# The last stage of a hybrid decoder layer, put into a written order: loads split off, output products by column halves

## The chip, the cores and the metric

The kernel runs on one core of a Trainium2 chip. The metric is the device time of one execution in microseconds (us). The kernel before was timed three times: median 2399.8 us, from 2398.44 to 2401.62. A further, profiled execution took 2395.87 us; the span of its trace, from the first instruction to the last, is 2394.1 us, and the 1.8 us between the two lie around the program.

## The reference, cut to what matters

One layer: RMSNorm, one input projection, two token mixers side by side (a chunked gated DeltaNet and a dilated windowed attention in three groups), gates, an output projection and the residual. Sequence 2048, model width 1024, everything float32. The last part, which the change touches:

```python
o_dn = rms_norm(o_dn, dn_norm_w[layer]) * jax.nn.silu(dn_z.reshape(B, T, DN_HEADS, HEAD_DIM))
y_dn = o_dn.reshape(B, T, DN_WIDTH) @ w_branch_dn[layer]
...
alpha = jax.nn.softmax(jnp.stack(lses, axis=0), axis=0)
o_swa = jnp.sum(alpha[..., None] * jnp.stack(outs, axis=0), axis=0).astype(x.dtype)
o_swa = o_swa * jax.nn.silu(swa_z.reshape(B, T, SWA_HEADS, HEAD_DIM))
y_swa = o_swa.reshape(B, T, SWA_WIDTH) @ w_branch_swa[layer]

g_dn, g_swa = jnp.split(gates, 2, axis=-1)
merged = jax.nn.sigmoid(g_dn) * y_dn + jax.nn.sigmoid(g_swa) * y_swa
x = x + merged @ w_out[layer]
```

## The kernel before, in words

Every large product is done in three matmuls: each float32 operand is split into a high part, rounded to the fp32r format (a ScalarE copy), and a low part, the remainder (a subtract on VectorE or GpSimd), and high times high, low times high and high times low are summed in PSUM. A **split** of a weight piece is therefore two instructions: `w_split` has the copy at L942 (ACT) and the subtract at L944 (DVE, or POOL for some pieces).

The program has three long stretches. First the attention projections and the attention itself. Then the channel units (`cunits`, matmuls L524 to L526), with the DeltaNet inverse and scan laid between them; the last units write the gates to DRAM (L915, L916). Then the **last stage**, from 2011 us on, in `run`: eight blocks of 256 tokens. A block has two parts:

- **branch products** (`fin_y`, eight times, m = 0 to 7, 24 matmuls of 256 columns each, L997 to L999) into a PSUM tile `mm`, of which there are three buffers. What follows each is called its **tail**: gates times sums (L1001, DVE, which also frees the PSUM buffer), the two branches added (L1003, POOL), the high part of the sum (`mh`, L1004, ACT) and its low part (`ml`, L1005, POOL). The gates come by a load `gt`, three buffers.
- **output products** (`fin_out`, four times: two tiles of 128 tokens by two halves of 512 columns, 24 matmuls of 512 columns each, L1014 to L1016), then the residual (L1020, DVE) and the store. Their step k reads `mh` and `ml` of branch product m = k.

Beside them run the preparations for the next block: for each tile of 128 tokens the **merge** (`combine`, L954 to L966: nine small and large DVE steps with one ACT step L956 between) of the three attention groups from a load `oc` of 780 KB with one buffer, and four times `o_prep`: a transpose on PE (L981), a product with the gate path `z` (L982, DVE) and its split (L985 ACT, L986 POOL).

The weights: 16 pieces of the branch weights are loaded and split near the end of the last channel unit (`tail`). 16 pieces of the output weight follow: they take the place of the activations that the last channel unit reads, so they are split from 2012 us on. They come in the order (k0 = 0, m = 0), (k0 = 4, m = 0), (k0 = 0, m = 1) and so on; here p0 to p15. A piece holds 512 rows by 128 columns: `fin_out` of the left half reads p0 to p7 and starts with the even ones, that of the right half p8 to p15. `take(n)` loads n pieces and splits those that are more than three loads old.

`at(d, f)` runs f after d further **hooks**; a hook comes after every sixth matmul of a unit or an output product, and twice in a branch product. It is a place in the program. For the attention (`swa`) the order written is the order run on PE, ACT, DVE and POOL (`manual_schedule`). All that comes later, the last stage too, is handed to a scheduler, which sets the order on every engine. The DMA queue on SP is ordered by it throughout that part.

## Time and profile before

| what | before |
|---|---|
| median of three runs | 2399.8 us |
| profiled execution; its span | 2395.87 us; 2394.1 us |
| PE busy | 2350.5 us (98%) |
| DVE, ACT, POOL busy | 1169.7, 856.6, 824.0 us |
| DMA moved | 307.30 MB, mean 128 GB/s |

PE is TensorE's matmuls, PEld its weight loads, DVE VectorE, ACT ScalarE, POOL GpSimd, SP the engine that issues the DMAs. Times in a row of the timeline are counted from the start of the span: start, length, engine, line, instruction, and in brackets the idle time before it with what ended it. L1014 is line 1014 of the kernel. A matmul's row is longer than its step: the next one starts before it ends.

### The profile page before, as it was taken

The page shows a single profiled execution, that of the slowest core. Times are in us where ns is not written, and L with a number is a line of the kernel's source. Part 1 is how long each engine was busy: PE and PEld are TensorE (multiplying, and loading weights), DVE is VectorE, ACT ScalarE, POOL GpSimd, SP SyncE. Part 2 cuts the span into 40 slices and gives each one's busy share as a digit, 9 for nine tenths or more (in the row PEclk, how much of TensorE's full clock was granted, in tenths as well). Part 3 has the DMA queues.
Part 4 walks back from the last instruction along what each step waited for, and adds up shares of the span by engine and source line. Part 5 has one row for each costly group of instructions (what it writes and reads, how often), then busy time and mean ns, then how long its engine had stood idle before and what let it go on. Part 6 is the DMA issues. An engine that isn't in the chain of part 4 may idle for free.

```text
span 2394.1 us, 40632 instructions
## 1 busy us (share of the span) xinstructions
PE 2350.5 (98%) x13640; PEld 2136.8 (89%) x13640; DVE 1169.7 (49%) x2819; ACT 856.6 (36%) x3021; POOL 824.0 (34%) x1803
## 2 busy tenths in 40 slices
PE   8999999999999999999999999999999999999999
PEld 7899999999999999988777878888888878889988
DVE  5543344334434434344666666999344433454431
ACT  6433333444434444334665662111233313111110
POOL 6633333333333334301442451101233212433441
PEclk9999999999999999999999999999999999999999
DMA  8443344333333335233454443222567645555442
GB/s 283 156 115 111 107 122 120 104 101 108 109 97 111 111 91 128 85 94 103 126 128 117 117 106 118 68 75 75 191 203 207 184 150 158 155 175 161 147 141 75
DMA packets 378808, 307.30 MB, mean 128 GB/s; under 512 B 61352, under 2 KB 345320, under 8 KB 378216
## 3 DMA queue, kind: packets, MB, share of 16 engines
q1 hardware_dynamic: 378312, 304.64, 43.5%
q8 instruction: 108, 1.77, 0.3%
q14 instruction: 100, 0.82, 0.1%
q10 hardware_dynamic: 288, 0.07, 0.0%
HBM read 187.92 MB, written 116.69 MB: 127 GB/s over the span
## 4 chain that ended last, share of the span: by engine, by line
PE 86%; DMA 4%; DVE 3%; POOL 3%; ACT 2%; issue 2%; SPq 0%; ACTq 0%; DVEq 0%; POOLq 0%
PE mm L238 10%; PE mm L240 10%; PE mm L239 10%; PE mm L524 9%; PE mm L526 9%; PE mm L525 9%; PE mm L1014 2%; PE mm L1016 2%; PE mm L1015 2%; PE mm L997 2%; PE mm L999 2%; PE mm L998 2%; DMA gcb<-gcscr 2%; PE po L333 2%; PE tp L290 2%
## 5 line engine op out<-in xcount | busy, mean ns | idle before, releaser
L238 PE MATMUL mm<-wh,hh 128*128 128x384 f32 (+1 forms) x1536 | 554.4, 361 | 6.1 <-ACT hh L131 2.7
L240 PE MATMUL mm<-wh,hl 128*128 128x384 f32 (+1 forms) x1536 | 519.3, 338 | 2.7 <-DVE hl L135 2.7
L239 PE MATMUL mm<-wl,hh 128*128 128x384 f32 (+1 forms) x1536 | 517.8, 337 | 0.7 <-DVE wl L79 0.6
L524 PE MATMUL mm<-hh,wh 128*128 128x512 f32 x1152 | 464.8, 403 | 0.0
L526 PE MATMUL mm<-hh,wl 128*128 128x512 f32 x1152 | 454.5, 395 | 0.0
L525 PE MATMUL mm<-hl,wh 128*128 128x512 f32 x1152 | 453.1, 393 | 0.0
L238 PEld LDWEIGHTS mm<-wh,hh 128*128 128x128 f32 x1536 | 289.6, 189 | 10.5 <-ACT wh L78 4.3
L240 PEld LDWEIGHTS mm<-wh,hl 128*128 128x128 f32 x1536 | 288.9, 188 | 4.1 <-DVE hl L135 4.1
L239 PEld LDWEIGHTS mm<-wl,hh 128*128 128x128 f32 x1536 | 290.5, 189 | 1.7 <-DVE wl L79 1.1
L526 PEld LDWEIGHTS mm<-hh,wl 128*128 128x128 f32 x1152 | 217.3, 189 | 47.3
L524 PEld LDWEIGHTS mm<-hh,wh 128*128 128x128 f32 x1152 | 217.6, 189 | 43.0
L525 PEld LDWEIGHTS mm<-hl,wh 128*128 128x128 f32 x1152 | 217.8, 189 | 41.2
L263 DVE SCALAR_TENSOR_TENSOR rec<-mm,st,wqk 128x128 f32<-128x128 f32 x384 | 116.7, 346 | 264.4 <-POOL st L255 239.4
L79 POOL TENSOR_TENSOR wl<-raw,wh 128x512 fp32r<-128x512 f32 (+1 forms) x73 | 104.2, 1439 | 409.4 <-ACT wh L78 409.2
L317 ACT ACTIVATE p<-sc,ol 128x128 f32<-128x128 f32 (+1 forms) x192 | 82.0, 427 | 315.8 <-DVE ol L315 273.3
L253 POOL TENSOR_SCALAR st<-st 128x2 f32<-128x2 f32 x192 | 37.7, 196 | 400.9 <-ACT rec L249 399.5
L249 ACT ACTIVATE rec<-mm 128x128 f32<-128x128 f32 x384 | 102.4, 272 | 185.3 <-PE mm L240 171.3
L997 PE MATMUL mm<-oh,hh 128*128 128x256 f32 x512 | 143.8, 281 | 3.1 <-DVE gt L1001 2.9
L999 PE MATMUL mm<-oh,hl 128*128 128x256 f32 x512 | 142.9, 279 | 0.0
L998 PE MATMUL mm<-ol,hh 128*128 128x256 f32 x512 | 142.9, 279 | 0.0
L629 DVE SCALAR_TENSOR_TENSOR acc<-xr,cw,acc 128x512 f32<-128x512 f32 x144 | 121.7, 845 | 41.9 <-ACT acc L627 37.7
L255 POOL TENSOR_TENSOR st<-st,mhalf 128x2 f32<-128x2 f32 x192 | 134.7, 702 | 16.0
(243 smaller groups left out, 4283.8 us busy)
## 6 DMA issues: line engine op xcount, KB each, us to landing
rscr<-rec SPq DMA_DIRECT2D x192, 192.0 KB, 1.9
raw<-in_w_in_dram SPq DMA_DIRECT2D x138, 256.0 KB, 3.0
qk<-rscr SPq DMA_DIRECT2D x192, 128.0 KB, 2.2
gscr<-gt SPq DMA_DIRECT2D x64, 256.0 KB, 2.4
gt<-gscr SPq DMA_DIRECT2D x64, 256.0 KB, 3.4
oscr<-ol SPq DMA_DIRECT2D x192, 65.0 KB, 2.0
oc<-oscr SPq DMA_DIRECT2D x16, 780.0 KB, 5.2
v<-rscr SPq DMA_DIRECT2D x192, 64.0 KB, 2.0
```

The source lines that it names most:

```text
L238: nc.tensor.matmul(pr[:, :w], a, wh[:, k, :w], start=(k == 0), stop=False)
L239: nc.tensor.matmul(pr[:, :w], a, wl[:, k, :w], start=False, stop=False)
L240: nc.tensor.matmul(pr[:, :w], b, wh[:, k, :w], start=False, stop=(k == KT - 1))
L255: nc.gpsimd.tensor_tensor(out=st[:, 2:4], in0=st[:, 0:2], in1=self.mhalf[:, 0:2], op=ALU.pow)
L263: nc.vector.scalar_tensor_tensor(out=qk[:, j, :], in0=pr[:, j * P:(j + 1) * P], scalar=st[:, 2 + j:3 + j], in1=s["w"][2][:, j, :], op0=ALU ...
L524: nc.tensor.matmul(pr, wh[:, k, :], a, start=(k == 0), stop=False)
L525: nc.tensor.matmul(pr, wh[:, k, :], b, start=False, stop=False)
L526: nc.tensor.matmul(pr, wl[:, k, :], a, start=False, stop=(k == KT - 1))
L629: nc.vector.scalar_tensor_tensor(out=acc, in0=xr[:, j:j + 512], scalar=w[:, j:j + 1], in1=acc, op0=ALU.mult, op1=ALU.add)
L997: nc.tensor.matmul(o, self.wbh[:, k, ms], oh[:, k, :], start=(k == b * 4), stop=False)
L998: nc.tensor.matmul(o, self.wbh[:, k, ms], ol[:, k, :], start=False, stop=False)
L999: nc.tensor.matmul(o, self.wbl[:, k, ms], oh[:, k, :], start=False, stop=(k == b * 4 + 3))
```

## The change

Six edits in the last stage and just ahead of it.

1. The loop over the eight blocks stands in a `manual_schedule`: on PE, ACT, DVE and POOL the order written is the order run. SP is left to the scheduler.
2. The load `oc` is issued by `o_load`, and the merge follows four hooks later (`merge`); the load of `z` has a function of its own (`z_load`); the load of the gates is issued one branch product ahead (`g_load`).
3. `take` in block 0: 2, 2, 1, 1, 1, 1, 1, 1 pieces after the eight branch products and 3 before each output product (before: 3, 3, 3, 3, 2, 2, 0, 0).
4. The output products run over column halves outside and token tiles inside.
5. The merges of a block stand at hooks 6 and 12 (block 0: at 10 and 16).
6. The first four `o_prep`, among the channel units, come four hooks (24 matmuls) later.

What it computes is the same, and so is the number of instructions on each engine. Lines shift: L1001, L1003, L1004, L1005 become L1013, L1015, L1016, L1017; L997 to L999 become L1009 to L1011; L1014 to L1016 become L1026 to L1028; the merge is L952 to L964, and L981, L982, L985, L986 are L987, L988, L991, L992. L942 and L944 stay.

```diff
@@ o_load, z_load, o_prep
         od = fp.tile([P, H, P], F32, name="od", bufs=2)
         nc.sync.dma_start(od.rearrange("p h c -> p (h c)"), dr(self.odn, t * P * 512, [[512, P], [1, 512]]))
-        x[t] = (od, self.combine(t))
+        oc = fp.tile([P, G, H, 130], F32, name="oc", bufs=1)
+        nc.sync.dma_start(oc.rearrange("p g h c -> p (g h c)"), dr(self.oscr, ...))
+
+        def merge():
+            x[t] = (od, self.combine(t, oc))
+        self.at(4, merge)
+
+    def z_load(self, t, b, x):
+        z = x["z", t, b] = self.fp.tile([P, H, P], F32, name="z", bufs=2)
+        self.nc.sync.dma_start(z, dr(self.zscr, b * 4 * P * T + t * P, [[T, P], [P * T, 4], [1, P]]))
...
@@ g_load, fin_y
+    def g_load(self, j):
+        nb, m = divmod(j, 8)
+        if j < 64:
+            gt = self.gts[j] = self.fp.tile([P, 2, 256], F32, name="gt4", bufs=3)
+            self.nc.sync.dma_start(gt, dr(self.gscr, m * P * T + nb * 256, [[T, P], [8 * P * T, 2], [1, 256]]))
+
     def fin_y(self, nb, m, oh, ol, mh, ml):
-        gt = fp.tile([P, 2, 256], F32, name="gt4", bufs=3)
-        nc.sync.dma_start(gt, dr(self.gscr, ...))
+        self.g_load(nb * 8 + m + 1)
+        gt = self.gts.pop(nb * 8 + m)
...
@@ o_start
+            if ("z", t, b) not in x:
+                self.at(max(d + 2 * j - 3, 1), lambda t=t, b=b: self.z_load(t, b, x))
             self.at(d + 2 * j, lambda t=t, b=b: self.o_prep(t, b, x, oh, ol))
...
@@ start_fin
-            self.at(12, lambda: xo.update(o0=self.o_start(0, xo)))
+            self.at(11, lambda: self.z_load(0, 0, xo))
+            self.at(12, lambda: self.z_load(0, 1, xo))
+            self.at(16, lambda: xo.update(o0=self.o_start(0, xo)))
...
@@ the last stage
+        self.gts = {}
+        with pinned(False):
+            self.g_load(0)
+            for nb in range(nbk):
...
+                if nb + 1 < nbk:
+                    d = 0 if nb else 4
+                    self.at(2 + d, lambda: self.o_load(2 * nb + 2, xo))
+                    self.at(8 + d, lambda: self.o_load(2 * nb + 3, xo))
...
+                for m in range(8):
+                    self.fin_y(nb, m, oh, ol, mh, ml)
+                    take((2, 2, 1, 1, 1, 1, 1, 1)[m])
+                if nb + 1 < nbk:
+                    oh, ol = self.o_start(nb + 1, xo, 0 if nb else 4)
                 for half in range(2):
-                    take(8)
-                    self.fin_out(t, half, mh, ml)
-            self.flush()
+                    for t in (2 * nb, 2 * nb + 1):
+                        take(3)
+                        self.fin_out(t, half, mh, ml)
+                self.flush()
```

How the instructions move on the engines that wait for each other, in three places.

**VectorE in block 0.** Rows are in the engine's order; `gt_...` names the branch product in the order of its number, `hl<-raw` is the low part of a weight piece. Before, from the second piece of the output weight on:

```order
L944 TENSOR_TENSOR hl<-raw_22152,hh 128x4x128
L944 TENSOR_TENSOR hl<-raw,hh 128x4x128 x2
L1001 SCALAR_TENSOR_TENSOR gt_22119<-gt_22119,mm 128x512
L944 TENSOR_TENSOR hl<-raw_22195,hh 128x4x128
L944 TENSOR_TENSOR hl<-raw,hh 128x4x128
L1001 SCALAR_TENSOR_TENSOR gt_22156<-gt_22156,mm 128x512
```

Now, from the first branch product's tail to the first merge of the block:

```order
L1013 SCALAR_TENSOR_TENSOR gt_22119<-gt_22119,mm 128x512
L1013 SCALAR_TENSOR_TENSOR gt_22123<-gt_22123,mm 128x512
L944 TENSOR_TENSOR hl<-raw,hh 128x4x128
L1013 SCALAR_TENSOR_TENSOR gt_22158<-gt_22158,mm 128x512
L944 TENSOR_TENSOR hl<-raw_22156,hh 128x4x128
L1013 SCALAR_TENSOR_TENSOR gt_22195<-gt_22195,mm 128x512
L944 TENSOR_TENSOR hl<-raw,hh 128x4x128
L952 TENSOR_REDUCE cs<-oc 128x4
```

and from the end of the second merge on:

```order
L961 TENSOR_TENSOR oc<-oc,cs 128x4x128 x3
L963 TENSOR_TENSOR osw<-oc 128x512
L964 TENSOR_TENSOR osw<-osw,oc 128x512
L1013 SCALAR_TENSOR_TENSOR gt_22357<-gt_22357,mm 128x512
L944 TENSOR_TENSOR hl<-raw,hh 128x4x128 x2
L944 TENSOR_TENSOR hl<-raw_22437,hh 128x4x128
```

Before, pieces were split ahead of the first tail and in pairs between tails, and the three merges that come next in the program (the third but for its last two steps) stood ahead of all of these rows. Now one piece stands between two tails, and the two merges stand in the row as well, the second ahead of the tail of m = 7 (`gt_22357`) and of p6, the first row behind it.

**ScalarE at the end of block 0's branch products.** `mh<-gt_...` is the high part of a branch product, `hh<-raw` that of a weight piece. Before:

```order
L942 ACTIVATE hh<-raw_22377 128x4x128
L1004 ACTIVATE mh<-gt_22285 128x256
L1004 ACTIVATE mh<-gt_22324 128x256
L1004 ACTIVATE mh<-gt_22387 128x256
L1004 ACTIVATE mh<-gt_22418 128x256
```

Now:

```order
L1016 ACTIVATE mh<-gt_22318 128x256
L942 ACTIVATE hh<-raw_22265 128x4x128
L954 ACTIVATE cs<-cs 128x12
L1016 ACTIVATE mh<-gt_22357 128x256
L942 ACTIVATE hh<-raw 128x4x128
L942 ACTIVATE hh<-raw_22353 128x4x128
```

Before, all 16 pieces stood ahead of the high part of m = 4. Now p5 (`raw_22265`) stands between those of m = 6 and m = 7, and p6 (the next `raw`) and p7 (`raw_22353`) behind that of m = 7.

**TensorE among the channel units**, at the fourth of the first transposes. Before:

```order
L524 MATMUL mm<-hh,wh_20966 128x512
L525 MATMUL mm<-hl,wh_20966 128x512
L526 MATMUL mm<-hh,wl_20967 128x512
L981 MATMUL tp<-ident,osw 128x128 x4
L524 MATMUL mm<-hh,wh_21415 128x512
```

Now:

```order
L524 MATMUL mm<-hh,wh_21415 128x512
L525 MATMUL mm<-hl,wh_21415 128x512
L526 MATMUL mm<-hh,wl_21416 128x512
L987 MATMUL tp<-ident,osw 128x128 x4
L524 MATMUL mm<-hh,wh_21415 128x512
```

It stood in front of a channel unit's first matmul and stands now behind that unit's 24th; each of the four transposes moved back by 24 matmuls. Nothing else moved on TensorE ahead of the last stage.

More of the change, by code (lines that the diff above doesn't have):

```diff
@@ L944, in w_split, with combine @@
         eng.tensor_tensor(out=lv, in0=raw, in1=hv.bitcast(F32), op=ALU.subtract)
-    def combine(self, t):
+    def combine(self, t, oc):
         nc, fp, V = self.nc, self.fp, self.nc.vector
-        oc = fp.tile([P, G, H, 130], F32, name="oc", bufs=1)
-        nc.sync.dma_start(oc.rearrange("p g h c -> p (g h c)"), dr(self.oscr, t * P * G * H * 130, [[G * H * 130, P], [1, G * H * 130]]))
         sm = fp.tile([P, 4, 12], F32, name="cs", bufs=1)
@@ L972, in o_load @@
         nc.sync.dma_start(od.rearrange("p h c -> p (h c)"), dr(self.odn, t * P * 512, [[512, P], [1, 512]]))
-        x[t] = (od, self.combine(t))
+        oc = fp.tile([P, G, H, 130], F32, name="oc", bufs=1)
+        nc.sync.dma_start(oc.rearrange("p g h c -> p (g h c)"), dr(self.oscr, t * P * G * H * 130, [[G * H * 130, P], [1, G * H * 130]]))
+        def merge():
[4 more added lines that the diff above has]
+        self.nc.sync.dma_start(z, dr(self.zscr, b * 4 * P * T + t * P, [[T, P], [P * T, 4], [1, P]]))
     def o_prep(self, t, b, x, oh, ol):
         nc, fp = self.nc, self.fp
-        z = fp.tile([P, H, P], F32, name="z", bufs=2)
-        nc.sync.dma_start(z, dr(self.zscr, b * 4 * P * T + t * P, [[T, P], [P * T, 4], [1, P]]))
+        z = x.pop(("z", t, b))
         pt = self.ps.tile([P, 512], F32, name="tp", bufs=2)
@@ L986, in o_prep @@
         nc.gpsimd.tensor_tensor(out=lv, in0=z, in1=hv.bitcast(F32), op=ALU.subtract)
+    def g_load(self, j):
[3 more added lines that the diff above has]
+            self.nc.sync.dma_start(gt, dr(self.gscr, m * P * T + nb * 256, [[T, P], [8 * P * T, 2], [1, 256]]))
     def fin_y(self, nb, m, oh, ol, mh, ml):
         nc, fp = self.nc, self.fp
-        gt = fp.tile([P, 2, 256], F32, name="gt4", bufs=3)
-        nc.sync.dma_start(gt, dr(self.gscr, m * P * T + nb * 256, [[T, P], [8 * P * T, 2], [1, 256]]))
+        self.g_load(nb * 8 + m + 1)
+        gt = self.gts.pop(nb * 8 + m)
         pr = self.ps.tile([P, 512], F32, name="mm", bufs=3)
@@ L1114, in run @@
         nbk = T // 256
-        for nb in range(nbk):
-            mh = self.lp.tile([P, KT, 256], F32R, name="mh", bufs=1)
-            ml = self.lp.tile([P, KT, 256], F32R, name="ml", bufs=1)
-            if nb + 1 < nbk:
-                d = 0 if nb else 8
-                self.at(4 + d, lambda: self.o_load(2 * nb + 2, xo))
-                self.at(10 + d, lambda: self.o_load(2 * nb + 3, xo))
-            for m in range(8):
-                self.fin_y(nb, m, oh, ol, mh, ml)
-                take((3, 3, 3, 3, 2, 2, 0, 0)[m])
-            if nb + 1 < nbk:
-                oh, ol = self.o_start(nb + 1, xo, 0 if nb else 6)
-            for t in (2 * nb, 2 * nb + 1):
+        self.gts = {}
+        with pinned(False):
+            self.g_load(0)
+            for nb in range(nbk):
+                mh = self.lp.tile([P, KT, 256], F32R, name="mh", bufs=1)
+                ml = self.lp.tile([P, KT, 256], F32R, name="ml", bufs=1)
+                if nb + 1 < nbk:
+                    d = 0 if nb else 4
+                    self.at(2 + d, lambda: self.o_load(2 * nb + 2, xo))
+                    self.at(8 + d, lambda: self.o_load(2 * nb + 3, xo))
+                    if nb:
+                        self.at(13, lambda: self.z_load(2 * nb + 2, 0, xo))
+                        self.at(15, lambda: self.z_load(2 * nb + 2, 1, xo))
+                for m in range(8):
[3 more added lines that the diff above has]
+                    oh, ol = self.o_start(nb + 1, xo, 0 if nb else 4)
                 for half in range(2):
-                    take(8)
-                    self.fin_out(t, half, mh, ml)
-            self.flush()
+                    for t in (2 * nb, 2 * nb + 1):
+                        take(3)
+                        self.fin_out(t, half, mh, ml)
+                self.flush()
         fst.close()
```

## The prediction

> **What bounds the kernel now.** I read the head of the page first, then who waited for whom on PE, then a table by windows, then PE's timeline at the places found.
>
> ```profile
> span 2394.1 us, 40632 instructions
> PE 2350.5 (98%) x13640; PEld 2136.8 (89%) x13640; DVE 1169.7 (49%) x2819; ACT 856.6 (36%) x3021; POOL 824.0 (34%) x1803
> ```
>
> PE is the bound, and the change leaves its instructions as they are. So only the time in which PE stands or runs slowly can move. From 1890 us on, PE's waits are three:
>
> ```profile
> PE tp L981 <- DVE osw L966: 3.1, 1, 3.1
> PE mm L997 <- DVE gt L1001: 2.9, 3, 1.6
> PE mm L1014 <- ACT mh L1004: 2.0, 3, 1.1
> ```
>
> ```profile
> core 0: us, PE busy (x) PEld busy (x) DVE busy (x) ACT busy (x) POOL busy (x), PEclk, DMA share, GB/s
> 1920.00:1926.00 6.00, 6.00 (x17) 4.85 (x18) 1.09 (x2) 2.67 (x5) 4.86 (x4) 0.51 0.73 237
> 2011.00:2037.50 26.50, 23.44 (x191) 22.59 (x190) 14.22 (x18) 12.47 (x22) 12.76 (x13) 1.00 0.79 223
> 2046.00:2052.00 6.00, 5.96 (x14) 4.58 (x15) 0.69 (x1) 0.00 (x0) 0.74 (x1) 0.50 0.52 169
> 2068.00:2114.00 46.00, 46.00 (x305) 42.01 (x304) 23.60 (x42) 6.19 (x14) 17.66 (x20) 1.00 0.58 178
> ```
>
> ```profile
> 1916.40 0.40 PE L526 MATMUL mm<-hh,wl 128*128 128x512 f32 x1
> 1919.89 1.08 PE L981 MATMUL tp<-ident,osw 128*128 128x128 f32 x4 [3.09 <-DVE osw L966]
> 2011.03 0.28 PE L997 MATMUL mm<-oh,hh 128*128 128x256 f32 x1
> 2037.77 0.39 PE L1014 MATMUL mm<-hh,mh 128*128 128x512 f32 x1
> 2038.00 0.39 PE L1015 MATMUL mm<-hl,mh 128*128 128x512 f32 x1
> 2046.04 0.80 PE L1014 MATMUL mm<-hh,mh 128*128 128x512 f32 x1 [1.09 <-ACT mh L1004]
> 2067.89 0.28 PE L997 MATMUL mm<-oh,hh 128*128 128x256 f32 x1
> 2114.17 0.28 PE L997 MATMUL mm<-oh,hh 128*128 128x256 f32 x1
> 2136.79 0.60 PE L981 MATMUL tp<-ident,od 128*128 128x128 f32 x4
> 2137.15 0.48 PE L1014 MATMUL mm<-hh,mh 128*128 128x512 f32 x1
> ```
>
> To be seen: block 0 runs from 2011.03 to 2067.89, 56.86 us; block 1 ends at 2114.17, 46.28 us with PE busy throughout and the clock at 1.00. Block 0 loses 10.6 us. Among the channel units the fourth transpose comes 3.09 us late, and after it the clock is 0.51 for 6 us. At full clock a 512-column step is 0.23 us (2037.77 to 2038.00), so 6 us hold 26; at half clock 14 ran (2046 to 2052). Each such phase costs 12 x 0.23 = 2.8 us. All that can be won is 10.6 + 3.09 + 2.8 = 16.5 us.
>
> **The first transposes, 24 matmuls later.** The wait is for a merge, here the undisturbed one and the last steps of the disturbed one:
>
> ```profile
> 1903.84 0.17 DVE L954 TENSOR_REDUCE cs<-oc 128x4 f32<-128x12 f32 x1 [3.72 <-DMA oc<-oscr]
> 1904.51 0.18 DVE L957 TENSOR_TENSOR cs<-cs,oc 128x12 f32<-128x12 f32 x1 [0.28 <-ACT cs L956]
> 1905.35 1.90 DVE L963 TENSOR_TENSOR oc<-oc,cs 128x512 f32<-128x512 f32 x3
> 1907.88 0.69 DVE L966 TENSOR_TENSOR osw<-osw,oc 128x512 f32<-128x512 f32 x1
> ...
> 1915.43 2.98 DVE L963 TENSOR_TENSOR oc<-oc,cs 128x512 f32<-128x512 f32 x3
> 1919.05 0.69 DVE L966 TENSOR_TENSOR osw<-osw,oc 128x512 f32<-128x512 f32 x1
> ```
>
> A merge takes 1903.84 to 1908.57, 4.73 us. PE asks 24 x 0.23 = 5.5 us later than it does now; the merge was 3.1 us late. The wait goes, and with it the half clock: -5.9 us. What is late next is the third transpose: its PSUM buffer is freed by the first product L982, which now stands behind the merge. It would be asked for at 1913.4 (1916.40 less 13 steps) + 5.5 = 1918.9; the second merge starts at 1913.4 when its load lands, ends at 1918.1 undisturbed (POOL has its splits of the preparations now behind it), and the product takes 0.75: 1918.9. I take no wait; with 2.98 in place of 1.90 it is 1.1 us.
>
> **Block 0.** Here the order becomes a chain. A branch product's tail, seen where nothing held it up, and the split of a piece:
>
> ```profile
> 2044.05 0.69 DVE L1001 SCALAR_TENSOR_TENSOR gt<-gt,mm 128x512 f32<-128x512 f32 x1 [4.73 <-DMA gt<-gscr]
> 2044.82 0.72 POOL L1003 TENSOR_TENSOR gt<-gt 128x256 f32<-128x256 f32 x1 [0.43 <-DVE gt L1001]
> 2045.57 0.42 ACT L1004 ACTIVATE mh<-gt 128x256 fp32r<-128x256 f32 x1 [1.99 <-POOL gt L1003]
> 2137.05 0.69 DVE L1001 SCALAR_TENSOR_TENSOR gt<-gt,mm 128x512 f32<-128x512 f32 x1 [2.14 <-POOL ml L1005]
> ```
>
> ```profile
> L944 DVE TENSOR_TENSOR hl<-raw,hh 128x512 fp32r<-128x512 f32 x15 | 13.3, 890 | 14.1 <-ACT hh L942 14.0
> L942 ACT ACTIVATE hh<-raw 128x512 fp32r<-128x512 f32 x22 | 13.9, 631 | 15.1 <-DMA raw<-in_w_out_dram 11.0 <-DMA raw<-in_w_branch_swa_dram 3.9
> L944 POOL TENSOR_TENSOR hl<-raw,hh 128x512 fp32r<-128x512 f32 x7 | 9.1, 1303 | 15.6 <-ACT hh L942 15.6
> ```
>
> From the DVE step's start (2044.05) to the end of `mh` (2045.99) is 1.94 us; an engine starts 0.03 (ACT behind POOL), 0.05 (PE behind ACT, 2046.04) or 0.08 us (POOL behind DVE) after the one it waits for. In the written order ACT copies a piece only behind the `mh` of the tail before it, and DVE subtracts that piece ahead of the next tail. One round is 1.94 + 0.63 + 0.03 + 0.89 = 3.49 us; PE makes a branch product in 22.62 / 8 = 2.83 (2114.17 to 2136.79). DVE falls behind, and the two merges come on top.
>
> The walk, from PE's first matmul, tail of m ready at 2.83(m + 1) + 0.26 (block 1's last at 2137.05, 22.88 behind its start): m = 1 starts at 5.92; p0 done 9.41; m = 2; p1 done 12.90; m = 3; p2 done 16.39; first merge to 21.12; m = 4 from 21.12. Its PSUM buffer is that of m = 7, which PE wants at 19.80 and gets at 21.87: 2.07 us of wait, m = 7 ends at 24.70. The `mh` of m = 4 ends at 23.06, the copy of p3 at 23.69, its POOL subtract (1.30 and 0.08 to start) at 25.07. POOL reaches m = 5 only now: `mh` 1.17 later, 26.24; copy of p4 26.87, subtract 27.79; m = 6, p5: 31.28; second merge to 36.01 (its load was free to start at 21.1 and is long there); m = 7: `mh` at 37.95; copy of p6 at 38.58. The first output product needs that copy for its first matmul. It starts at 38.63, not at 24.70: 13.93 us. Its second matmul needs the subtract, 39.56 against 39.06: 0.50. p8 to p15 are split beside the first two output products of 5.5 us each; by the same steps p14 is ready within half a microsecond of its use in the third. I take 0 there, at most 1. On SP the load of the second merge waits for the end of the first (21.1), with the gates of m = 7 and p9 queued behind it: wanted at 36.0 and by the third output product, landing 5 us after issue, they hold nothing. Sum: 2.07 + 13.93 + 0.50 = 16.5, and a phase of half clock behind so long a stand, 2.8: 19.3 us. Block 0 would take 46.28 + 19.3 = 65.6 where it took 56.9: +8.7.
>
> By the Trainium skill, "TensorE: Matmul & The Clock Gate", section "What's actually happening", an idle window of some 3.4 us drops the clock to half and a busy one of 3.4 us restores it. By its 3.4 us the phase would cost 1.7 and the sum be 1.1 us less; the trace's phases (clock 0.51 and 0.50 over 6 us) decide.
>
> Bounds of block 0. Lower: splits at 0.69, the length of an undisturbed one on DVE (like L966's 0.69), take 0.2 off each of six, -1.2, and half a phase -1.4: +6.1. Upper: both merges disturbed like the one at 1915.43, +1.1 each, the six subtracts by as much again as the mean lies over 0.69, +1.2, and a second phase, +2.8: +14.9. I take the means, as the trace gives them for this very stage.
>
> **Blocks 1 to 6.** No splits; DVE has 23.60 of 46 us. But merges stand at fixed places, and tails go one behind the other through POOL:
>
> ```profile
> 2119.19 0.73 POOL L1003 TENSOR_TENSOR gt<-gt 128x256 f32<-128x256 f32 x1 [16.86 <-DVE gt L1001]
> 2121.15 0.73 POOL L1003 TENSOR_TENSOR gt<-gt 128x256 f32<-128x256 f32 x1
> 2122.41 0.74 POOL L1005 TENSOR_TENSOR ml<-gt,mh 128x256 fp32r<-128x256 f32 x1 [0.53 <-ACT mh L1004]
> ```
>
> A tail holds POOL for 1.96 us, its last one for 2.00. The first merge stands behind the tail of m = 1, its ACT step behind that tail's `mh` (7.86). From there a merge takes 0.28 and 4.06 us (L957 to the end of L966 above): it ends at 12.20. The tails of m = 2, 3, 4 start on POOL at 12.97, 14.93, 16.89; `mh` of m = 4 is done at 18.06, the second merge behind it at 22.40. Then m = 5 frees its PSUM buffer at 23.15. The first output product wants that buffer at 22.98 (2137.15): 0.17 us. The low part of m = 7, done at 29.09, it wants in its last step, 23 x 0.23 + 2 transposes of 0.36 + 0.17 later: 29.2, just in time. Six blocks: +1.0 us; the lower bound is 0, where the stand ends in a step's own slack. The loads apart from the work cost nothing either: they land under DVE's other work, and the gates' loads come earlier than they did. Column halves move no instruction on PE but the order of four products, 0.
>
> **Sum.** -5.9 + 8.7 + 1.0 = +3.8 us. The profiled execution, 2395.87 (span 2394.1 and 1.8 around it), becomes 2399.7. It lies 3.9 under the median; the same step on the median gives **2403.6 us**.
>
> **Rivals.**
>
> *Each of blocks 1 to 6 loses much more (slower).* The walk leaves no slack there. For it, two adds of a merge, POOL beside them, and the landing of the load `oc`:
>
> ```profile
> 2093.59 1.76 DVE L965 TENSOR_TENSOR osw<-oc 128x512 f32<-128x512 f32 x1
> 2095.38 1.66 DVE L966 TENSOR_TENSOR osw<-osw,oc 128x512 f32<-128x512 f32 x1
> 2093.50 2.98 POOL L986 TENSOR_TENSOR ol<-z,oh 128x512 fp32r<-128x512 f32 x2
> DMA to landing us min/median/max: 4.6/5.2/7.0
> ```
>
> Beside POOL's subtract the merge's adds take 1.76 and 1.66 where they took 0.69: +2.0 us. The load of the second merge starts at 12.2; at 7.0 us it lands at 19.2, 1.1 behind 18.06. It decides from any lateness on: 1.1 to 2.0 per block, six blocks, +7 to +12: 2410 to 2416. Against it: POOL has no such subtract there by the walk. Chance 0.15.
>
> The Trainium skill, "GPSIMD Engine Reference", section "Specifications", says that GpSimd shares its SBUF interfaces with VectorE and contends with its instructions of two SBUF inputs. By that rule the adds suffer only beside POOL, as the rows at 2093 do.
>
> *Amount of work counts, not order (faster).* DVE has in block 0, up to the last tail, 8 x 0.69 + 5 x 0.89 + 2 x 4.73 = 19.4 us of work and 22.6 us of time. If it keeps up, PE waits only from m = 7 to the copy of p6: 0.26 + 1.94 + 0.63 = 2.8. Then -5.9 - 10.6 + 2.8 = -13.7: 2386. If half of the chain's 16.5 us comes out, -5.9 - 10.6 + 8.2 + 2.8 = -5.5: 2394. Against it: each round crosses three engines in a fixed order. Chance 0.15.
>
> *The first transposes still wait.* If the second merge stays disturbed and PE stands long enough for half clock, the -5.9 shrinks to -5.9 + 1.1 + 2.8 = -2.0: 2407.5. The row at 1915.43 speaks for it; that POOL and L982 are out of its way speaks against. Chance 0.1.
>
> **How the numbers follow.** The forecast has 0.6, with its own range from the bounds, 2400 (0.0: -5.9 + 6.1) to 2410 (-5.9 + 14.9 + 1.0). The range 2393 to 2412 leaves out the fast end of the faster rival and the slow end of the first. A measurement here tells 0.2%, 4.8 us, from no change. Faster by more (under 2395): most of the second rival, 0.12. Slower by more (over 2404.6): 0.24 of the forecast's 0.6, the first rival and most of the third, 0.46. Same: 0.42.
>
> **What would show it.** In the profile after: no wait for L964 ahead of a transpose, clock 1.00 from 1920 to 1926; block 0 about 65 us, PE idle some 14 us ahead of the first output product with ACT's copy of a weight piece as the one that ends it, a clock of 0.5 behind it; a wait of 2 us ahead of m = 7 for DVE; blocks 1 to 6 at 46.3 to 46.5 us each. The prediction is wrong if DVE's tails of block 0 keep to 2.83 us, or if each later block loses half a microsecond or more.

## The result, and the profile after

The changed kernel takes 2405.8 us (median of seven runs), the kernel before beside it 2396.1: the ratio is 1.0037, with a 95% interval of 1.0025 to 1.0048. It is slower by 0.37%, 9.7 us, where +3.8 had been forecast. The profiled execution took 2408.2 us, 12.4 more than the one before.

The head of the page after:

```profile
span 2406.5 us, 40630 instructions
PE 2347.9 (98%) x13640; PEld 2135.3 (89%) x13640; DVE 1166.3 (48%) x2819; ACT 852.7 (35%) x3021; POOL 818.2 (34%) x1803
```

PE has the same 13640 matmuls; DVE, ACT and POOL work no longer than they did. The time is PE's standing. Whom PE waited for from 1890 us on (total, times, longest):

```profile
PE mm L1026 <- ACT hh L942: 13.0, 1, 13.0
PE mm L1026 <- DVE gt L1013: 3.7, 6, 0.6
PE mm L1009 <- DVE gt L1013: 1.0, 1, 1.0
PE mm L1027 <- DVE hl L944: 0.8, 1, 0.8
```

The wait for the merge ahead of the first transposes is gone. In its place are one wait of 13.0 us, for the copy of a weight piece, and six of 0.6, one in each of blocks 1 to 6. On PE's timeline they stand here, with the start of block 0 first and those of blocks 1 and 2 between:

```profile
2010.91 0.28 PE L1009 MATMUL mm<-oh,hh 128*128 128x256 f32 x1
2031.85 0.38 PE L1009 MATMUL mm<-oh,hh 128*128 128x256 f32 x1 [0.99 <-DVE gt L1013]
2047.93 0.79 PE L1026 MATMUL mm<-hh,mh 128*128 128x512 f32 x1 [13.00 <-ACT hh L942]
2063.81 0.50 PE L1027 MATMUL mm<-hl,mh 128*128 128x512 f32 x1 [0.82 <-DVE hl L944]
2075.09 0.28 PE L1009 MATMUL mm<-oh,hh 128*128 128x256 f32 x1
2122.23 0.28 PE L1009 MATMUL mm<-oh,hh 128*128 128x256 f32 x1
2146.06 0.47 PE L1026 MATMUL mm<-hh,mh 128*128 128x512 f32 x1 [0.61 <-DVE gt L1013]
```

Block 0 takes 2075.09 - 2010.91 = 64.2 us (56.9 before); block 1 takes 47.14, where it took 46.28, and so do all six. The table by windows shows the clock (the column behind POOL's):

```profile
1920.00:1926.00 6.00, 6.00 (x33) 4.72 (x30) 5.15 (x11) 1.70 (x5) 0.50 (x1) 1.00 0.71 196
...
2035.20:2038.60 3.40, 0.00 (x0) 0.00 (x0) 1.39 (x2) 0.94 (x2) 1.65 (x3) 1.00 0.59 159
2038.65:2052.28 13.63, 4.30 (x9) 3.10 (x10) 8.41 (x16) 3.65 (x8) 3.94 (x5) 0.50 0.62 177
2052.32:2055.70 3.38, 3.38 (x16) 2.77 (x15) 0.00 (x0) 0.00 (x0) 0.00 (x0) 1.00 0.73 207
```

At the first transposes the clock now stays at 1.00, and PE makes 33 steps in 6 us where it made 17. Four microseconds into the stand of 13 us it goes to half, for 13.65 us from 2038.64 on, and PE works in the last 4.4 of them.

**Not all of the 12.4 us between the two profiles is the change's.** PE's first 8100 matmuls, up to 1404 us, are the same in both programs and in the same order, yet those from 1086 us on took longer. Waits of PE from 1086 to 1410 us on ACT's `st`, in the first profile before, in the profile after, and in a second profile of the unchanged kernel (e8, below):

```profile
PE tp L663 <- ACT st L668: 8.4, 6, 2.9
```
```profile
PE tp L663 <- ACT st L668: 11.1, 6, 3.2
```
```profile
PE tp L663 <- ACT st L668: 11.9, 7, 3.3
```

From matmul 6600 to 8100 it is 317.7, 322.6 and 321.7 us. The first profile before had a short one. Matmul by matmul, the last stage stands so against the two profiles of the kernel before:

| stretch | before, first | before, second | after | forecast |
|---|---|---|---|---|
| matmul 10500 to block 0 | 150.8 | 149.7 | 144.95 | 144.9 |
| block 0 | 56.9 | 53.9 | 64.2 | 65.6 |
| blocks 1 to 6, each | 46.28 | 46.28 | 47.15 | 46.45 |
| block 7 | 44.2 | 44.2 | 44.2 | 44.2 |

Against the first, the change makes -5.9 + 7.3 + 5.2 = +6.6 us; against the second, -4.8 + 10.3 + 5.2 = +10.7. The medians differ by 9.7.

### The profile page after: what moved, and what is told of

It reads as the page before. It is cut to its first block, busy times and chain, and to the rows that moved or that the text cites. A ratio compares the mean times of both kernels' runs of the same rounds, so it can differ in the third digit from the quotient of the medians.

```text
span 2406.5 us, 40630 instructions
## 1 busy us (share of the span) xinstructions
PE 2347.9 (98%) x13640; PEld 2135.3 (89%) x13640; DVE 1166.3 (48%) x2819; ACT 852.7 (35%) x3021; POOL 818.2 (34%) x1803
## 4 chain that ended last, share of the span: by engine, by line
PE 86%; DVE 4%; DMA 3%; POOL 3%; ACT 2%; issue 2%; SPq 0%; DVEq 0%; ACTq 0%; POOLq 0%
PE mm L238 10%; PE mm L240 10%; PE mm L239 10%; PE mm L524 9%; PE mm L526 9%; PE mm L525 9%; PE mm L1026 2%; PE mm L1027 2%; PE mm L1028 2%; DMA gcb<-gcscr 2%; PE mm L1009 2%; PE mm L1011 2%; PE mm L1010 2%; PE po L333 2%; PE tp L290 2%
## 5 line engine op out<-in xcount | busy, mean ns | idle before, releaser
L1009 PE MATMUL mm<-oh,hh 128*128 128x256 f32 x512 | 143.4, 280 | 1.0 <-DVE gt L1013 1.0
L1011 PE MATMUL mm<-oh,hl 128*128 128x256 f32 x512 | 142.9, 279 | 0.0
```

The lines of the kernel that those rows point to most:

```text
L1009: nc.tensor.matmul(o, self.wbh[:, k, ms], oh[:, k, :], start=(k == b * 4), stop=False)
L1011: nc.tensor.matmul(o, self.wbl[:, k, ms], oh[:, k, :], start=False, stop=(k == b * 4 + 3))
```

## The experiments

Each experiment was compared with the kernel before on the same chip; that one's median was 2397 to 2399 us there (2396.1 beside the changed kernel). Block times are read from PE's first branch product of a block to that of the next.

| run | median us | ratio to before (95%) | block 0 | blocks 1 to 6 |
|---|---|---|---|---|
| changed kernel | 2405.8 | 1.0037 (1.0025 to 1.0048) | 64.2 | 47.15 |
| e1 transposes later only | 2392.5 | 0.9979 (0.9971 to 0.9988) | 55.6 | 46.28 to 46.32 |
| e2 no fixed order | 2392.5 | 0.9977 (0.9968 to 0.9986) | 54.6 | 45.86 to 46.99 |
| e3 second merge one tail later | 2408.8 | 1.0054 (1.0040 to 1.0067) | 64.2 | 47.33 to 47.74 |
| e4 second merge behind all tails | 2402.8 | 1.0024 (1.0014 to 1.0034) | 64.5 | 46.36 to 46.67 |
| e5 low part one tail later | 2425.5 | 1.0116 (1.0102 to 1.0130) | 64.4 | 49.8 to 52.0 |
| e6 block 0's merges behind its tails | 2403.8 | 1.0020 (1.0009 to 1.0030) | 61.3 | 47.15 to 47.18 |
| e7 order repaired | 2393.5 | 0.9981 (0.9973 to 0.9990) | 55.0 | 46.35, block 1 47.6 |
| e9 e5 with four gates' buffers | 2399.5 | 1.0009 (0.9998 to 1.0020) | 63.4 | 46.28 |
| e10 e7, first merge between tails | 2391.6 | 0.9965 (0.9953 to 0.9978) | 55.8 | 46.34 to 46.35 |
| e11 all of these | 2388.5 | 0.9956 (0.9938 to 0.9973) | 49.3 | 46.35, block 1 47.8 |

### e1: the first transposes alone

```diff
 (kernel before)
-            self.at(12, lambda: xo.update(o0=self.o_start(0, xo)))
+            self.at(16, lambda: xo.update(o0=self.o_start(0, xo)))
```

> The kernel before with one number changed: the preparations of block 0 (its four transposes among the channel units) are asked for at hook 16 in place of 12; no fixed order, no loads apart, blocks 0 to 7 as before. Theory: the wait of 3.09 us for the merge and the half clock behind it (2.8 us) go, so the stretch from PE's matmul number 10500 to its first branch product (before 1860.21 to 2011.03, 150.8 us; changed kernel 1865.96 to 2010.91, 144.9 us) is 145 us here too, clock 1.00 from 1920 to 1926, and the time is 5.9 us under the kernel before: ratio 0.9975. Block 0 stays near 57 us and blocks 1 to 6 at 46.3. Rival (the transposes still wait, because without a load of z apart from its work they wait for that load or for the merges that the scheduler orders): 148 to 151 us, gain 0 to 3 us, ratio 0.9988 to 1.0.

The stretch to block 0 took 144.9 us, the clock was 1.00, and the time is 4.8 us (2.9 to 7.0 by the interval) under the kernel before. So this part is worth what was forecast against the first profile, 5.9; against the second profile before, in which the half clock behind the wait lasted 3.41 us and not 6.83, it is worth 4.8. Loads apart from their work are not needed for it.

### e2: the same edits without the fixed order

```diff
-        with pinned(False):
+        if True:
             self.g_load(0)
```

> The changed kernel without its fixed order: the last stage goes to the scheduler as in the kernel before, all other edits stay (loads apart, column halves, later transposes, the counts of pieces). Theory (the order, not the amount of work, makes block 0 a chain): the same copies, subtracts, tails and merges are there, yet block 0 takes 47 to 57 us in place of 64.18, and blocks 1 to 6 take 46.3 in place of 47.15. Against the changed kernel 7 to 17 us from block 0 and 5 from blocks 1 to 6: 12 to 22 us less, against the kernel before -3 to -10 us: ratio 0.996 to 0.999. Rival (column halves and the counts of pieces cost the time, since half 0 needs eight pieces ahead of the first output product): block 0 stays at 60 us or more whoever orders it, ratio 0.999 to 1.003.

Block 0 took 54.6 us, between the kernel before's two profiles (53.9 and 56.9), and blocks 1 to 6 took 46.3 on the mean; the ratio is e1's. The column halves, the loads apart and the counts of pieces therefore cost nothing that can be measured: the loss, block 0's and that of blocks 1 to 6, comes with the written order.

### e3 and e4: where the second merge of blocks 1 to 6 stands

```diff
 (e3)
-                    self.at(8 + d, lambda: self.o_load(2 * nb + 3, xo))
+                    self.at(10 if nb else 12, lambda: self.o_load(2 * nb + 3, xo))
 (e4)
+                    self.at(14 if nb else 12, lambda: self.o_load(2 * nb + 3, xo))
```

> The changed kernel with the load and so the merge of the second tile of blocks 1 to 6 two hooks later: the merge then stands behind the tail of m = 5 and not ahead of it; block 0 untouched. Theory (tails and both merges are one chain through DVE, POOL and ACT that is too long for a block as a whole: eight rounds of about 1.97 us behind 5.9, and two merges of 4.8): the PSUM buffer of m = 5 is free in time and the wait of 0.61 us ahead of the first output product goes, but the low part of m = 7 comes as late as before while PE wants it 0.8 us earlier, so a wait of 0.5 to 0.8 us appears in the last three steps of the first output product: blocks 1 to 6 stay at 47.0 to 47.1 us, ratio to the kernel before 1.003 to 1.004. Rival (only the PSUM buffer of m = 5 is short, the rest has slack): blocks 1 to 6 fall to 46.3 us, 5.2 us less than the changed kernel, ratio 1.001 to 1.002.

> The changed kernel with the merge of the second tile of blocks 1 to 6 behind the tail of m = 7, within the first output product; block 0 untouched. Theory (the chain of tails is too long only because two merges stand in it): no wait for a branch product's buffer or for a low part is left, blocks 1 to 6 take 46.3 us each in place of 47.15, 5.2 us less than the changed kernel, ratio to the kernel before 1.001 to 1.002. The fourth preparation has its merge by 2 to 3 us ahead of its transposes. Rival (blocks 1 to 6 are longer for another reason, such as the transposes that stand among their output products or the order of the halves): they stay at 47.1 us, or the wait moves to the transposes of the fourth preparation.

PE's waits in blocks 1 to 7, first in e3, then in e4:

```profile
PE mm L1026 <- ACT mh L1016: 3.1, 6, 0.6
```
```profile
PE tp L987 <- DVE z L988: 0.4, 2, 0.2
```

In e3 the wait for the buffer of m = 5 is gone and comes back, as large, within the first output product: for the `mh` of m = 7. The blocks take 47.3 to 47.7 us, a little over the 47.0 to 47.1 that the theory gave. Making room at one point of a chain that is too long moves the wait and saves nothing. In e4 one merge leaves the chain, and the wait goes; the rest, 0.1 to 0.4 us a block, is in steps around the fourth preparation, which e4's rival had named.

### e5 and e9: what the walk of blocks 1 to 6 had missed

The rows of one merge in block 2 of the changed kernel, DVE, ACT and POOL in order of time:

```profile
2128.69 0.17 DVE L952 TENSOR_REDUCE cs<-oc 128x4 f32<-128x12 f32 x1
2128.85 0.73 POOL L1015 TENSOR_TENSOR gt<-gt 128x256 f32<-128x256 f32 x1 [0.82 <-DVE gt L1013]
2128.90 0.73 DVE L953 TENSOR_TENSOR cs<-cs,oc 128x12 f32<-128x12 f32 x1
2129.62 0.42 ACT L1016 ACTIVATE mh<-gt 128x256 fp32r<-128x256 f32 x1 [2.41 <-POOL gt L1015]
2129.94 0.20 ACT L954 ACTIVATE cs<-cs 128x12 f32<-128x12 f32 x1
2130.11 0.74 POOL L1017 TENSOR_TENSOR ml<-gt,mh 128x256 fp32r<-128x256 f32 x1 [0.53 <-ACT mh L1016]
2130.17 0.72 DVE L955 TENSOR_TENSOR cs<-cs,oc 128x12 f32<-128x12 f32 x1 [0.55 <-ACT cs L954]
2130.93 0.17 DVE L956 TENSOR_REDUCE cs<-cs 128x4 f32<-128x12 f32 x1
```

Two products of 12 columns take 0.73 and 0.72 us, as long as the POOL step of 256 columns beside each, and end with it (2129.63 and 2129.58; 2130.89 and 2130.85). The first is hidden: the exponent waits for `mh` anyway. The second (L955) is on the chain, 0.54 us more than the 0.18 of the walk, in both merges. The steps of one input, L952 and L956, ran beside no POOL step here. In e10, below, one did (there the merge's lines are three higher, and L946 is the subtract of a weight piece):

```profile
2040.48 0.16 DVE L955 TENSOR_REDUCE cs<-oc 128x4 f32<-128x12 f32 x1
2040.68 1.09 DVE L956 TENSOR_TENSOR cs<-cs,oc 128x12 f32<-128x12 f32 x1
```
```profile
2040.23 1.50 POOL L946 TENSOR_TENSOR hl<-raw,hh 128x512 fp32r<-128x512 f32 x1 [0.82 <-ACT hh L942]
```

It took 0.16 us; the product behind it took 1.09 and ended with POOL's step (2041.77 and 2041.73). By the Trainium skill, "GPSIMD Engine Reference", section "Specifications", it is instructions of VectorE with two SBUF inputs that contend with GpSimd; these rows agree. e5 takes POOL's subtract out of the way, by putting it one tail later:

```diff
-        nc.gpsimd.tensor_tensor(out=ml[:, m, :], in0=gt[:, 0, :], in1=mh[:, m, :].bitcast(F32), op=ALU.subtract)
+        def low():
+            nc.gpsimd.tensor_tensor(out=ml[:, m, :], in0=gt[:, 0, :], in1=mh[:, m, :].bitcast(F32), op=ALU.subtract)
+        if m:
+            self.low()
+        self.low = low
+        if m == 7:
+            low()
```

> The changed kernel with POOL's subtract of the low part (`ml`) of m put behind POOL's add of m + 1, that of m = 7 last; nothing else moves. In the changed kernel the small DVE steps of a merge in blocks 1 to 6 take 0.73 and 0.72 us where one seen alone takes 0.18, and each ends as POOL's subtract beside it ends. Theory (DVE's two-input steps wait for POOL's, and this 0.5 us per merge is what the walk of blocks 1 to 6 missed): behind the tail ahead of a merge POOL now stands idle, the product L955 of the changed kernel takes 0.2 us in place of 0.72, a merge is 0.5 us shorter, the tails are shorter too, the wait of 0.61 us ahead of the first output product is gone, blocks 1 to 6 take 46.3 us in place of 47.15. Ratio to the kernel before 1.000 to 1.002. Rival (these steps are long for another reason, such as the wait for ACT's exponent inside them, or the wait is the fixed order's whatever POOL does): L955 stays at 0.7 us and blocks 1 to 6 at 47 us.

The merge got shorter as expected (L955 took 180 ns on the mean), and the kernel 20 us slower. DVE's tail of m = 4 in block 1 of e5:

```profile
2090.22 0.69 DVE L1013 SCALAR_TENSOR_TENSOR gt<-gt,mm 128x512 f32<-128x512 f32 x1 [4.63 <-DMA gt<-gscr]
```

The subtract reads `gt`, so the buffer of the gates was held one tail longer; with three buffers the load of later gates started late, and DVE stood 4.63 us for it. A cover had been lost that neither theory had priced. e9 gives it a fourth buffer:

```diff
-            gt = self.gts[j] = self.fp.tile([P, 2, 256], F32, name="gt4", bufs=3)
+            gt = self.gts[j] = self.fp.tile([P, 2, 256], F32, name="gt4", bufs=4)
```

> The kernel of e5 (low part one tail later) with four buffers for the gates `gt` in place of three. In e5 the row of L955 fell to 0.18 us as expected, yet blocks 1 to 6 took 49.8 to 52.0 us: DVE's tail of m = 4 waits 4.63 us for its gates to land, since the low part, read one tail later, holds a gates' buffer one tail longer. Theory (both are true: POOL's subtract beside the merge costs 0.5 us per merge, and in e5 the buffer cost more than that): with a fourth buffer the waits for gates are gone, L955 stays at 0.18, the wait ahead of the first output product too, blocks 1 to 6 take 46.3 us; ratio to the kernel before 1.000 to 1.002. Rival (the later low part itself is late, or merges of 4.3 us are still too long): blocks 1 to 6 stay at 47 us or more.

DVE's groups of the two products over blocks 1 to 6, in the changed kernel and then in e9 (busy us, mean ns of one):

```profile
L955 DVE TENSOR_TENSOR cs<-cs,oc 128x12 f32<-128x12 f32 x12 | 8.6, 721 | 6.6 <-ACT cs L954 6.6
L953 DVE TENSOR_TENSOR cs<-cs,oc 128x12 f32<-128x12 f32 x12 | 8.5, 707 | 0.4
```
```profile
L953 DVE TENSOR_TENSOR cs<-cs,oc 128x12 f32<-128x12 f32 x12 | 6.2, 516 | 0.4
L955 DVE TENSOR_TENSOR cs<-cs,oc 128x12 f32<-128x12 f32 x12 | 2.2, 181 | 5.3 <-ACT cs L954 5.3
```

L955 fell from 721 to 181 ns, PE has no wait left in blocks 1 to 7, and blocks 1 to 6 take 46.28 us, to the hundredth what they took before. With merges and DVE's tails where they were, the 0.87 us of each block are gone. Two merges at 0.54 us would be enough for that; but POOL's tails also got shorter, since its subtract no longer waits for the `mh` just made, and the two were not parted.

### e6, e7, e10, e11: what block 0's chain is made of

e6 takes only the two merges out of the stretch ahead of block 0's first output product:

```diff
-                    self.at(2 + d, lambda: self.o_load(2 * nb + 2, xo))
-                    self.at(8 + d, lambda: self.o_load(2 * nb + 3, xo))
+                    self.at(2 if nb else 18, lambda: self.o_load(2 * nb + 2, xo))
+                    self.at(8 if nb else 22, lambda: self.o_load(2 * nb + 3, xo))
...
-                    oh, ol = self.o_start(nb + 1, xo, 0 if nb else 4)
+                    oh, ol = self.o_start(nb + 1, xo, 0 if nb else 8)
```

> The changed kernel with the two merges of block 0 and their loads behind its tails, among the output products (loads at hooks 18 and 22 of block 0 in place of 6 and 12, so merges at 22 and 26, preparations four hooks later); splits and blocks 1 to 6 untouched. Theory (block 0 is one chain; each piece of it that leaves the stretch ahead of the first output product takes its whole length off PE's wait): tails keep to rounds of 3.24 us, the tail of m = 7 starts at 25.3 in place of 34.5 us behind the block's start, the first output product at 28.0 in place of 37.0, no wait ahead of m = 7, one phase of half clock: block 0 takes 54 to 56 us in place of 64.2, and the time is 8 to 10 us under the changed kernel, ratio 0.999 to 1.001. Rival (it is the sum of DVE's work in block 0): the merges then hold up the subtracts of p8 to p15 and the preparations, PE waits in the third output product or at the start of block 1, block 0 and block 1 together stay at 109 us or more (changed kernel 111.3).

PE's waits in block 0 of e6:

```profile
PE mm L1026 <- ACT hh L942: 5.0, 1, 5.0
PE tp L987 <- DVE osw L964: 4.2, 1, 4.2
```

Half a hit. The first output product started 27.8 us behind the block's start in place of 37.0; the theory had said 28.0. Behind it the rival was right: the merges then made a transpose wait 4.2 us, with half clock after that, and block 0 kept 61.3 of 64.2 us, where the theory had 54 to 56 (with block 1 it is 108.5, just under the rival's 109). e7 then undoes the chain of splits and moves both merges:

```diff
-        eng.tensor_tensor(out=lv, in0=raw, in1=hv.bitcast(F32), op=ALU.subtract)
+        def low():
+            eng = nc.gpsimd if (k0 and m % 2) else nc.vector
+            eng.tensor_tensor(out=lv, in0=raw, in1=hv.bitcast(F32), op=ALU.subtract)
+        return low
...
+        lows = []
+
+        def lag():
+            while lows:
+                lows.pop(0)()
...
+                lag()
                 if pieces:
                     ahead.append(self.w_fin(*pieces.pop()))
                     if len(ahead) > keep:
-                        self.w_split(*ahead.pop(0))
+                        lows.append(self.w_split(*ahead.pop(0)))
+            if not late:
+                lag()
...
             self.g_load(0)
+            take(3)
...
-                    self.at(2 + d, lambda: self.o_load(2 * nb + 2, xo))
-                    self.at(8 + d, lambda: self.o_load(2 * nb + 3, xo))
+                    self.at(2 if nb else 17, lambda: self.o_load(2 * nb + 2, xo))
+                    self.at(13 if nb else 21, lambda: self.o_load(2 * nb + 3, xo))
...
-                    take((2, 2, 1, 1, 1, 1, 1, 1)[m])
+                    take((2, 2, 1, 1, 1, 1, 1, 1)[m], late=True)
...
-                    oh, ol = self.o_start(nb + 1, xo, 0 if nb else 4)
+                    oh, ol = self.o_start(nb + 1, xo, 2 if nb else 8)
```

(`lag` issues the subtract of the piece that was copied one tail earlier; `late` leaves a tail's last subtract to the next tail. `take(3)` ahead of the blocks brings the first splits to the tail of m = 0, where the changed kernel has its first at m = 1.)

In e7, e10 and e11 lines have moved: L1012 to L1014 are the branch products, L1016 is the DVE step of a tail, L1029 to L1031 are the output products (L1036 to L1038 in e11), L946 is the subtract of a weight piece, L955 to L967 are the merge, and L990, L991, L995 the transpose, the product and the subtract of a preparation.

> The changed kernel with its fixed order kept but the chain taken apart: in block 0 three pieces are loaded ahead of the first branch product, a piece's subtract stands one tail behind its copy, p6 and p7 are split by the tail of m = 6, and the two merges stand among the output products; in blocks 1 to 6 the second merge stands behind all tails, the preparations two hooks later. Theory: with no split's subtract behind the `mh` of the tail ahead of it, tails keep to PE's 2.83 us, no wait is over half a microsecond, no half clock in the last stage: block 0 takes 46.3 to 48.5 us, blocks 1 to 6 46.3 to 46.5. From block 0's start at 2011 that ends at 2387 us: 10 us under the kernel before, ratio 0.995 to 0.997. Rival (a fixed order always loses to the scheduler's here): block 0 stays above the 54.6 us that it takes without a fixed order, ratio above 0.998.

PE's waits in e7 from block 0's start to 2070 us, and the row of DVE that the longest goes back to:

```profile
PE tp L990 <- DVE z L991: 4.9, 1, 4.9
PE tp L990 <- DVE osw L967: 1.3, 1, 1.3
PE mm L1013 <- POOL ol L995: 1.0, 1, 1.0
```
```profile
2050.81 0.18 DVE L955 TENSOR_REDUCE cs<-oc 128x4 f32<-128x12 f32 x1 [4.86 <-DMA oc<-oscr]
```

Ahead of the first output product nothing is lost any more: it starts 22.61 us behind the block's start. The splits and tails are the same work, still in a fixed order. Three things differ: a subtract stands one tail behind its copy, the splits begin one tail earlier, and the merges stand behind. e6, which moved the merges alone, kept a wait of 5.0 us, so the other two took that away; they were not parted from each other. Behind the start of the output PE lost 8.6 us, since the second merge's load could start only when the first merge had freed the one buffer `oc` (it was issued at 2044.72 us; the first merge's last step ended at 2044.69). By its numbers e7 came out on the rival's side, 55.0 us for block 0 against 54.6 and a ratio of 0.9981; e11, also in a fixed order, shows that this is no rule. e10 puts the first merge back among the tails (loads at hooks 6 and 13, preparations two hooks earlier, and `take(2 - half)` for `take(3)` ahead of the output products):

> The kernel of e7 with the first merge of block 0 back among its branch products (load at hook 6, merge at hook 10), the load of the second at hook 13, its merge at 17, preparations two hooks earlier, and the last pieces spread over two output products. In e7 block 0 lost nothing ahead of its first output product (22.61 us) but 8.6 us behind it: 1.35 us for the first merge, 4.90 us for the second, whose load could start only when the first merge had freed `oc`, and the half clock behind that. Theory (that one buffer is what is left; with splits out of the chain a merge fits among the tails): block 0 takes 46.3 to 48.5 us, block 1 46.4, ratio to the kernel before 0.993 to 0.996. Rival (a merge among the tails makes the chain too long once more): PE waits for a PSUM buffer or for p6 ahead of the first output product by 2 us or more, block 0 50 to 55 us, ratio 0.997 to 0.999.

```profile
PE mm L1030 <- DVE hl L946: 3.0, 1, 3.0
PE mm L1012 <- DVE gt L1016: 1.9, 1, 1.9
PE mm L1030 <- POOL hl L946: 0.5, 1, 0.5
```

These are PE's waits in block 0 of e10. Its total, 55.8 us, is the rival's or worse, and the wait of 1.9 us for a tail is close to the rival's 2; the larger wait is neither's: the pieces left over, spread later, stood behind the second merge. The ratio, 0.9965, can hardly be told from e7's (the intervals overlap). Against the changed kernel block 0 is 8.4 us shorter, and blocks 1 to 6 are 4.8 shorter together. e11 takes each part from the kernel in which it worked (all pieces ahead of the first output product as in e7, the load of `oc` as in e10, the low part and four gates' buffers of e9, block 0's second merge at hook 23):

> The kernel of e10 with what e9 and e7 showed put in: the low part one tail later with four buffers for gates, all pieces left split ahead of the first output product as in e7, and the second merge of block 0 at hook 23, its load still at hook 13. In e10 block 0 took 55.8 us: PE waited 1.89 us ahead of m = 7 and 3.04 us in the third output product for the subtract of a piece that stood behind the second merge, then half clock. Theory (each wait of the last stage is a place in the order, and none is DVE's amount of work): the piece is in time as in e7, the merge has its load in time as in e10, no stand is over 1.5 us, no half clock: block 0 takes 46.3 to 49 us, 7 to 9 us under e10, ratio to the kernel before 0.992 to 0.995. Rival (DVE's work in block 0 is too much for 46 us in any order): a wait of 3 us or more turns up elsewhere, block 0 stays at 52 us or more, ratio 0.996 to 0.998.

PE's waits in all of e11's last stage:

```profile
PE mm L1012 <- DVE gt L1016: 1.0, 1, 1.0
PE mm L1013 <- POOL ol L995: 1.0, 1, 1.0
PE tp L990 <- DVE z L991: 0.5, 1, 0.5
PE mm L1037 <- POOL hl L946: 0.4, 1, 0.4
```

None is over 1.0 us, and the clock stays at 1.00 through the last stage. Block 0 takes 49.3 us, 0.3 over the expected end; block 1 pays 1.4, since the last preparation of block 0 is late (the wait for `ol`). At 2388.5 us it is 0.44% under the kernel before (0.27 to 0.62), which falls between the theory's range and the rival's. It is the lowest median here, though its interval overlaps e10's; with the same arithmetic as the changed kernel it is some 17 us under that one's median, taken on another chip.

### e8: the kernel before, once more

> The kernel before, unchanged, once more. Of the profiled executions so far, the stretch from PE's matmul number 6600 to 8100 (1086 to 1404 us) took 317.7 us in the kernel before and 321.1 to 323.2 in the five others, though its instructions are the same in all. Theory (this stretch varies from execution to execution, by whether PE's waits there reach half clock, and the first profile of the kernel before had a short one): 317 to 323 us here, nearer 321, and the last stage (blocks 0 to 7) the same to 0.5 us as in the first profile. Rival (the stretch is shorter in the kernel before for a reason in its program): 317.7 again, within 0.5.

The stretch from matmul 6600 to 8100 took 321.7 us, so its length varies and is no effect of the program (in the twelve other profiles it took 317.7 to 323.2). The second half of the expectation missed: block 0 took 53.9 us, not 56.9, with the same waits (2.9 and 1.7 us where there were 2.9 and 2.0). The clock shows why. It changes only at steps of 3.41 us (last section). Here are the steps in which PE had these waits, in the first profile and then in this one, where the block starts 4.4 us later:

```profile
2041.89:2045.30 3.41, 2.27 (x6) 0.76 (x5) 0.69 (x1) 0.42 (x1) 2.46 (x4) 1.00 0.49 140
```
```profile
2044.84:2048.25 3.41, 2.56 (x8) 0.98 (x7) 0.32 (x1) 0.83 (x2) 2.36 (x4) 1.00 0.36 99
2048.25:2051.66 3.41, 2.21 (x8) 1.27 (x8) 0.75 (x2) 0.42 (x1) 1.55 (x3) 1.00 0.46 131
```

In the first profile PE started five matmuls of 512 columns in the step (of the six, one began ahead of it), and half clock followed, from 2045.30 on for 6.83 us. Here the waits fell into two steps with seven starts each, and no half clock followed. The 56.9 us on which the forecast built was block 0 at its longer.

## Why the prediction came out as it did

The direction and the range held; the size did not: +3.8 forecast, +9.7 measured.

- **First transposes, -5.9.** Right to the tenth against the profile it was made from (150.8 to 144.95 us), and e1 alone shows it. No wait turned up at the third transpose; the nearest thing is 0.15 us at one step.
- **Block 0, +8.7 (65.6 us).** The mechanism was right: e2, without the order, does not have the loss, and the stretch ahead of the first output product gets shorter when the merges leave the chain (e6) and again when the subtracts do (e7). 64.2 us were measured. A round took 3.24 us, not 3.49:

```profile
2020.01 0.68 DVE L1013 SCALAR_TENSOR_TENSOR gt<-gt,mm 128x512 f32<-128x512 f32 x1
2022.51 0.81 DVE L944 TENSOR_TENSOR hl<-raw,hh 128x512 fp32r<-128x512 f32 x1 [1.82 <-ACT hh L942]
2023.25 0.67 DVE L1013 SCALAR_TENSOR_TENSOR gt<-gt,mm 128x512 f32<-128x512 f32 x1
```

  These are DVE's rows of one round in block 0: the subtract took 0.81, not the group's mean of 0.89, and an operation starts 0.07 us ahead of the end of the one in front (2023.25 against 2023.32). So PE waited 0.99 for m = 7 (2.07 forecast) and 13.00 for the copy of p6 (13.93). The phase of half clock cost about 2.0 us (4.4 us of work at 0.43 us a step, where full clock takes 0.23; 0.43 is 6 us by the 14 steps in the row at 2046 of the profile before), under the 2.8 taken. The prediction's estimate by the 3.4 us of the Trainium skill, "TensorE: Matmul & The Clock Gate", section "What's actually happening", was 1.7; here the phase lasted 13.65 us. The wait for p14, taken as 0, was 0.82 us. In all block 0 lost 64.2 - 46.3 = 17.9 us, where 19.3 had been forecast.
- **The base of block 0.** The gain or loss of a block was counted from one execution in which a phase of half clock followed waits of 1 us; in the next there was none, and block 0 was 3.0 us shorter. That makes the loss +10.3 in place of +7.3.
- **Blocks 1 to 6, +1.0: the term that was mis-sized.** The place was named (m = 5 frees its buffer too late for the first output product), and the wait stood exactly there. PE's idle row is 0.61 us, and each block is 0.87 longer, not 0.17: +5.2. By the prediction's own sign, half a microsecond or more in each later block, this part was wrong. The step that failed was to take a merge as "0.28 and 4.06 us" from one that stood beside an idle POOL. In the written order L955 stands beside POOL's subtract each time and takes 0.72 us. The prediction had said of the contention that POOL "has no such subtract there by the walk"; it had looked for the long subtract of the preparations and passed over the short one of the tail, which the walk itself put at that moment. e9 brings the 0.87 us back by moving that subtract; how much of it was L955 and how much POOL's own tails stays open.
- **The time itself.** 2405.8 us lies 2.2 from the forecast 2403.6, and that nearness is luck: the forecast started from three runs with a median of 2399.8, where seven give 2396.1. Against the second profile the change makes +10.7: 6.9 more than forecast, from blocks 1 to 6 (4.2), the base of block 0 (3.0) and that of the transposes (1.1), less 1.4 of block 0's chain.
- **Rivals.** The first had the place right, its mechanism half: two-input steps beside POOL, yet small ones, and 0.87 us where it gave 1.1 to 2.0. "Amount of work counts" fell for the stretch ahead of the output (in e6 DVE has two merges, 9.5 us, less to do there, and PE still waits 5.0) and holds in part behind it: in e6 the merges only moved the stand. "The first transposes still wait" fell with e1.

## What to carry to other kernels

A fixed order is priced as one chain: walk it with the durations that each step has beside its new neighbours, and not with those of the undisturbed row. Where two steps need each other across engines (copy here, subtract there), the second can be written one turn later, so that no engine stands in its queue for the other (e7 did so, and began the splits earlier too); then count how much longer its inputs' buffers are then held, since a buffer that is missing costs a whole load (20 us in e5 against 5 gained in e9). Take a second profile of the kernel before, where a term of a few microseconds rests on one: here two executions of one program differ by 3.0 us in a single block.

## What the runs showed of the hardware

- A DVE product of 12 columns, 0.18 us alone, took 0.72 beside a POOL step of 256 columns and 1.09 beside a longer one, and ended with it each time; how long POOL still ran, and not the product's size, set what it lost there.
- Phases of half clock begin and end on a grid of 3.41 us within an execution. In the profile after they start at 1168.24, 1222.86, 1390.11 and 2038.64 us, 16, 65 and 255 steps of 3.413 us behind the first; they last 3.41, 3.41, 3.41 and 13.65. PE resumed at 2047.93 and got full clock at 2052.30, the end of the first step of that grid in which it worked throughout. By the Trainium skill, "TensorE: Matmul & The Clock Gate", section "What's actually happening", an idle window of some 3.4 us halves the clock and a busy one restores it; the length agrees. But a step need not be empty to count as idle: in the last stage of all thirteen profiles half clock followed each of the 14 steps at full clock in which PE started at most five matmuls of 512 columns (or as many columns in smaller ones; some 15 fit at 0.23 us each), and none of the 1375 in which it started six or more. So the same waits brought a phase in one execution and none in the next (56.9 and 53.9 us for one block), by where they fell on the grid.
